# Sixteen more tokens gather their second products, ten pairs of chunks of v go unsplit, and one pool holds the PSUM banks

## The chip, the core and the metric

The kernel runs on one core of a Trainium2 chip. A core has a matrix engine (TensorE, PE in the profile), a vector engine (VectorE, DVE), a scalar engine (ScalarE, ACT), GpSimd (POOL) and a queue engine that only issues DMAs (SyncE, SP). Each engine works through its own list of instructions in order, and semaphores tie the lists together. The metric is the device time of one execution in microseconds, the median of the runs shown.

## What is computed

One layer of a decoder for 256 tokens of width 1024. A mixer (retention and block attention) comes first and isn't touched by the change. Behind it stands a layer of 16384 small experts, 8 heads with 16 experts each for every token:

```python
def peer(h, w_q, sub_keys, u_tab, v_tab):
    ...
    top_s, pos = lax.top_k(cand_s, PEER_TOPK)
    experts = jnp.take_along_axis(cand_i, pos, axis=-1)
    gates = jax.nn.softmax(top_s, axis=-1).astype(h.dtype)
    ...
        u = u_tab[ec]
        a = jax.nn.gelu(jnp.einsum('td,thkd->thk', hc, u), approximate=False)
        return jnp.einsum('thk,thkd->td', gc * a, v_tab[ec])
```

`u_tab` and `v_tab` have 16384 rows of 1024 numbers, in float32. The "first product" of a token and an expert is the dot product with a row of `u_tab`, the "second product" is the weight times a row of `v_tab`, added up over the experts.

## The kernel before

The span has three stages. Up to about 312 us stand the mixer, the projection to the queries and the first scores. Then come two passes over the expert tables in 128 chunks of 128 rows each, first over `u_tab` (312 to 689 us, the loop at L1173), then over `v_tab` (689 to 985 us, the loop at L1224). The order of every engine's instructions is the order in which the program is written, since a manual schedule is set (L76); pieces of side work (a list of generators) are handed out by small budgets per chunk.

**Three kinds of tokens.** The first 64 tokens (NG) gather both products: two partitions stand for a token, and 64 indirect DMAs (NJ) each fetch one row for each of the 128 partitions, 512 KB in all. The next 64 tokens (NX, four groups of 16, eight partitions a token) gather only their first products, with 64 more indirect DMAs; their weights are sent back to the token order through memory (`weights_x`, L965, and `back`, L976). The last 128 tokens gather nothing. So the pass over `u_tab` has NA = 128 columns of tokens, and the pass over `v_tab` has ND = 192.

**The pass over u.** For each chunk TensorE turns the chunk (L681, 8 transposes of 128x128 into PSUM tiles), ScalarE copies it out (L682), and TensorE multiplies it with the tokens (L1188, 8 products of 128 columns, float32). A float32 matmul of the program is two matmul instructions in the trace. `W`, a tile of 128 partitions by 128 chunks by ND tokens, takes the result. Beside this, one-hot factors for four tokens at a time are built on DVE (L1077, L1079) and ACT (L1083), TensorE multiplies them (L1117) into the gates of all experts, and these are multiplied into `W` (L1130, L1132). There are ND/4 = 48 such groups, 8 matmul instructions each. DVE also takes the dot products of the gathered rows (`dot_v`, L962), at `GATHER` or `GATHER_G` steps a chunk.

**The pass over v.** The products are to be exact to about float32, at the faster rate of the type fp32r. So each chunk of v is split in a high part (ACT, L143) and a low part (DVE, L144), and each pair of chunks of `W` in a high and a low part that stand side by side in `cw` (ACT L1161, DVE L1162). For each of eight blocks of 128 output columns, TensorE then does two matmuls: the high part of v with both parts of `W` (L1220, 2 x 192 = 384 columns) and the low part of v with the high part of `W` (L1221, 192 columns). The eight results stay in the eight PSUM banks during the whole pass. The split runs two chunks ahead; its tiles have four buffers. The raw chunks arrive in a ring of six buffers (`RAWS`) by DMAs that SP issues, each as soon as the split has freed its buffer. Beside this, `gather_step` (L1003) fetches rows of v by indirect DMA (L951, issued by POOL) and DVE adds them up with their weights (L1035), `GATHER_V` = 0.56 steps a chunk, with RING = 5 row buffers.

**The end.** The last two chunks are done block by block. Each block is added up (L1257, L1258), turned back (L1263, L1264), added to the residual (L1265, L1266) and written out (L1269, L1270).

**PSUM.** A pool of 4 tiles under each of two names serves up to 312 us (L82). It is closed there (L1062), and three new pools take its banks (L1064 to L1066): `acc` for the products, `gates` and `turn`. They are closed in turn at the end of the pass over u (L1211), and a pool of eight tiles takes over. A tile of a new pool has to wait until every tile that stood in its bank is free.

Of the kernel before, what the change touches and what calls it, by code (L numbers as in the profile page):

```python
# [22 lines left out]
P = 128  # L23
S = 256
# [46 lines left out]
def layer_kernel(ctx, tc, x, mix_norm_g, w_in, ret_w_branch, moba_q_gain, moba_k_gain, moba_w_branch,  # L71
# [10 lines left out]
    psum = {"acc": cps.enter_context(tc.tile_pool(name="ps", bufs=4, space=bass.MemoryType.PSUM))}  # L82
    psum["side"] = psum["acc"]
# [12 lines left out]
    raw_ring = rg.tile([P, RAWS, 1024], F32, name="raw_ring")  # L96
    raw_count = [0]
# [108 lines left out]
    def products(i):  # L206
        u, src, k0, n0 = pieces[i]
        hi, lo = splits.pop(i)
        kc = u["kc"]
        if k0 == 0:  # L210
            if u["before"]:
                u["before"]()
            u["o"] = [acc() for _ in range(2)]
        o = u["o"]
        lh, ll = u["lhs"]
        def parts(j):
            k, n = k0 + j, slice(j * 512, (j + 1) * 512)
            return k, lh[k // 4][:, k % 4, :], ll[k // 4][:, k % 4, :], hi[:, n], lo[:, n]

        if u["mode"] == "nat":  # L220
            for t in range(NT):
                s = slice(t * P, (t + 1) * P)
                for j in range(2):
                    k, xh, xl, wh, wl = parts(j)
                    T.matmul(o[t], xh[:, s], wh, start=(k == 0), stop=False)  # L225
                    T.matmul(o[t], xh[:, s], wl, start=False, stop=False)  # L226
                    T.matmul(o[t], xl[:, s], wh, start=False, stop=(k == kc - 1))  # L227
        else:
            for j in range(2):
                k, xh, xl, wh, wl = parts(j)  # L230
                for b in range(4):
                    s = slice(b * P, (b + 1) * P)
                    d = o[b // 2][:, (b % 2) * S:(b % 2 + 1) * S]
                    T.matmul(d, wh[:, s], xh, start=(k == 0 and b % 2 == 0), stop=False, skip_group_check=True)  # L234
                    T.matmul(d, wh[:, s], xl, start=False, stop=False, skip_group_check=True)  # L235
                    T.matmul(d, wl[:, s], xh, start=False, stop=(k == kc - 1), skip_group_check=True)  # L236
# [434 lines left out]
    def transpose_u(c):  # L671

        if c < NK and c % STEP == STEP - 1 and c // STEP < NPRE:
            u_T[c] = u_raw.pop(c)
        elif c < NK:
            r = u_raw.pop(c)
            u_T[c] = hi_tile(F32)
            for q in range(2):
                p = psum["turn"].tile([P, 512], F32, name="turn") if "turn" in psum else side()
                for k in range(4):  # L680
                    T.transpose(p[:, k * P:(k + 1) * P], r.rearrange("p (i k) -> p k i", k=KC)[:, 4 * q + k], ident)  # L681
                A.activation(u_T[c][:, 512 * q:512 * (q + 1)], p, AF.Copy)  # L682
# [32 lines left out]
    grow1 = [acc() for _ in range(2)]  # L715
# [249 lines left out]
    def weights_x():  # L965
# [37 lines left out]
    def gather_step():  # L1003
# [6 lines left out]
        if gs["dot"] < NU:  # L1010
# [17 lines left out]
        if gs["sum"] < gs["v"] and (gs["v"] - gs["sum"] == RING or gs["v"] == NJ):  # L1028
            j = gs["sum"]
            r = gs["rows"].pop(j)  # L1030
            if j == 0:
                gs["acc"] = cp.tile([P, D], F32, name="vacc", tag="h2")
                A.activation(gs["acc"], r, AF.Copy, scale=av[:, 0:1])
            else:
                V.scalar_tensor_tensor(gs["acc"], r, av[:, j:j + 1], gs["acc"], op0=OP.mult, op1=OP.add)  # L1035
# [57 lines left out]
    def dense_gates():  # L1093

        def columns(t):
            p = psum["turn"].tile([P, 512], F32, name="turn")
# [10 lines left out]
        for n0 in range(0, ND + 4 * LAG_G, 4):  # L1107
# [4 lines left out]
                columns(0)  # L1112
            if len(built) == LAG_G or (n0 >= ND and built):
                n1, oh = built.pop(0)
                p = psum["gates"].tile([P, 512], F32, name="gp")
                for j, (o2, o1) in enumerate(oh[0]):
                    T.matmul(p[:, j * P:(j + 1) * P], o2, o1, start=True, stop=True)  # L1117
# [55 lines left out]
    for c in range(NK):  # L1173
# [34 lines left out]
    product_evac(NK - 2, pa)  # L1208


    cps.close()  # L1211
    psum["acc"] = ctx.enter_context(tc.tile_pool(name="psv", bufs=KC, space=bass.MemoryType.PSUM))

    o = [acc() for _ in range(KC)]
    half = P - NG

    def block(b, c):
        vh, vl, w = cuts[c]
        n = slice(b * P, (b + 1) * P)
        T.matmul(o[b][:, :2 * ND], vh[:, n], w, start=(c == 0), stop=False, skip_group_check=True)  # L1220
        T.matmul(o[b][:, :ND], vl[:, n], w[:, :ND], start=False, stop=(c == NK - 1), skip_group_check=True)  # L1221

    cuts = {}
    for c in range(NK):  # L1224
        load_to(len(pieces) + NK + c + 2)
        cut_v(c + 2)
        if c % 2 == 0:
            cut_w(c + 2)
        cuts[c] = (*v_cut.pop(c), w_cut[c - c % 2][:, c % 2])
        if c < NK - 2:  # L1230
            for b in range(KC):
                block(b, c)
            del cuts[c]
        gather(GATHER_V)
        if c == NK - 8:
            while gs["sum"] < NJ:
                gather_step()

            r0 = tk.tile([P, D], F32, name="rows_")
# [4 lines left out]
            nc.gpsimd.dma_start(r0b[:half], x1d[NG:, 0, :])  # L1244
# [8 lines left out]
    back = {}  # L1253

    def add_up(b):
        lo = back[b] = hp_.tile([P, 2, 2 * P], F32, name="turned", tag="hl", bufs=2)
        A.activation(lo[:, 0, :ND], o[b][:, ND:2 * ND], AF.Copy)  # L1257
        V.tensor_tensor(lo[:, 1, :ND], lo[:, 0, :ND], o[b][:, :ND], op=OP.add)  # L1258

    def turn_back(b):  # L1260
        t = back.pop(b)
        n = slice(b * P, (b + 1) * P)
        T.transpose(o[b][:, :P], t[:, 1, :P], ident)  # L1263
        T.transpose(o[b][:half, P:2 * P], t[:, 1, P:ND], ident)  # L1264
        V.tensor_tensor(r1[:, n], r1[:, n], o[b][:, :P], op=OP.add)  # L1265
        V.tensor_tensor(r0b[:half, n], r0b[:half, n], o[b][:half, P:2 * P], op=OP.add)  # L1266
        if b in (3, 5, 7):
            d = slice({3: 0, 5: 512, 7: 768}[b], P * (b + 1))
            nc.sync.dma_start(out_flat[P:, d], r1[:, d])  # L1269
            (nc.scalar if b == 7 else nc.sync).dma_start(out_flat[NG:P, d], r0b[:half, d])  # L1270
# [62 lines left out]
```

## Time and profile before

| | |
|---|---|
| time, median of 3 runs | 993.85 us (991.02 to 995.42) |
| the profiled execution, its own time | 992.1 us |
| its span, from the first to the last instruction | 990.3 us |
| granted TensorE clock | 1.00 |
| busy: PE, DVE, ACT, POOL | 979.6, 802.9, 551.8, 336.8 us |
| moved by DMA | 309.94 MB, 313 GB/s over the span |

A view of the profile is a list of rows: an engine, a line of the program (L1220), what is written and read, how often, and how long. "Busy" for TensorE has to be read with care, since matmuls are pipelined and overlap: what counts is the distance from one start to the next. The chain of waits is the work that ended last, followed back from the last instruction to what released it. Starts are given in us from the start of the span.

### The profile page before, as it was taken

Reading aid. Unit: us, or ns where it says so; the run is one execution under the profiler, and the core shown is the slowest. Engines: PE = TensorE matmul, PEld = TensorE weight load, DVE = VectorE, ACT = ScalarE, POOL = GpSimd, SP = SyncE. Lnnn points to the kernel's source line nnn. Section 1 sums busy time; section 2 is a strip of 40 time slices with the busy share of each in tenths; the row PEclk is TensorE's granted clock in tenths of the full one; section 3 lists DMA queues with packets and bytes.
Section 4 is the critical chain, followed back from the end, with each engine's and each line's share of the span. In section 5 each row is a group of like instructions: output and inputs, shape, how many; then the busy total and the mean of one; then the engine's idle time right before and its main releaser. Section 6 shows DMA issues by size and latency. Waiting matters only on the chain.

```text
span 990.3 us, 19575 instructions
## 1 busy us (share of the span) xinstructions
PE 979.6 (99%) x7384; PEld 942.9 (95%) x7384; DVE 802.9 (81%) x1509; ACT 551.8 (56%) x992; POOL 336.8 (34%) x287
## 2 busy tenths in 40 slices
PE   9999999999998999999999999999999999999998
PEld 6887998998998999999999999999999999999997
DVE  6567665978679996999688898863999899999976
ACT  5544554535543545444577776986555555555553
POOL 2421000000203455343446565653444344444300
PEclk9999999999999999999999999999999999999999
DMA  8876777996798999999998888999999999999991
GB/s 304 239 198 188 234 226 205 285 305 204 246 375 330 402 352 343 347 363 394 373 342 316 346 333 337 332 390 320 352 360 347 365 363 346 372 351 347 354 284 48
DMA packets 105563, 309.94 MB, mean 313 GB/s; under 512 B 10956, under 2 KB 21093, under 8 KB 105342
## 3 DMA queue, kind: packets, MB, share of 16 engines
q1 hardware_dynamic: 64492, 184.69, 53.1%
q0 software_dynamic: 30240, 107.16, 29.7%
q10 hardware_dynamic: 10738, 16.85, 5.5%
q8 instruction: 58, 0.95, 0.4%
q14 instruction: 35, 0.29, 0.1%
HBM read 298.09 MB, written 12.09 MB: 313 GB/s over the span
## 4 chain that ended last, share of the span: by engine, by line
PE 92%; DVE 3%; DMA 2%; ACT 1%; issue 1%; POOL 0%; ACTq 0%; DVEq 0%; another core or an unknown queue 0%; POOLq 0%
PE acc L1188 21%; PE acc L1220 21%; PE turn L681 9%; PE acc L1221 9%; PE acc L234 4%; PE acc L235 4%; PE acc L236 4%; PE acc L225 4%; PE acc L227 4%; PE acc L226 4%; PE gp L1117 4%; PE side L586 1%; DMA rows<-in_peer_u_dram,eg 1%; DVE rows L962 1%; PE side L356 1%
## 5 line engine op out<-in xcount | busy, mean ns | idle before, releaser
L951 POOL DMA_INDIRECT rows<-in_peer_u_dram,eg x103 | 122.3, 1187 | 93.7 <-DVE rows L962 40.9
L951 POOL DMA_INDIRECT rows<-in_peer_v_dram,eg x51 | 89.3, 1752 | 105.3 <-DVE vacc L1035 100.0
L681 PE MATMUL turn<-ident,raw_ring 128*128 128x128 f32 x816 | 107.1, 274 | 0.0
L681 PEld LDWEIGHTS turn<-ident,raw_ring 128*128 128x128 f32 x816 | 98.7, 190 | 0.0
L962 DVE SCALAR_TENSOR_TENSOR rows<-rows,h 128x1024 f32<-128x1024 f32 x52 | 63.4, 1222 | 21.3 <-DMA rows<-in_peer_u_dram,eg 20.0
L1161 ACT ACTIVATE cw<-W 128x384 fp32r<-128x384 f32 x64 | 33.7, 526 | 81.9 <-PE acc L1221 62.1
L1035 DVE SCALAR_TENSOR_TENSOR vacc<-rows,av,vacc 128x1024 f32<-128x1024 f32 x50 | 64.0, 1280 | 0.0
L1162 DVE TENSOR_TENSOR cw<-W,cw 128x384 fp32r<-128x384 f32 x64 | 36.1, 564 | 20.1 <-ACT cw L1161 18.3
L1132 ACT ACTIVATE W<-gp 128x512 f32<-128x512 f32 (+17 forms) x48 | 33.1, 689 | 32.7 <-DVE W L1130 27.5
L1147 POOL TENSOR_TENSOR W<-W,gl 128x256 f32<-128x256 f32 (+16 forms) x29 | 23.4, 808 | 69.2 <-ACT gl L1146 59.5
L1077 DVE TENSOR_TENSOR oh_buf<-niota,tT 128x512 f32<-128x512 f32 x48 | 34.4, 717 | 7.7 <-ACT tT L1099 7.7
L1130 DVE TENSOR_TENSOR W<-gp,W 128x280 f32<-128x280 f32 (+16 forms) x32 | 29.7, 929 | 4.4 <-PE gp L1117 2.8
L1083 ACT ACTIVATE oh_more<-oh_more,tT 128x128 f32<-128x128 bf16 x96 | 32.1, 428 | 0.0
L1083 ACT ACTIVATE oh_buf<-oh_more,tT 128x128 f32<-128x128 bf16 x96 | 32.1, 428 | 0.0
L541 POOL DMA_DIRECT2D x1d<-xt x1 | 0.7, 657 | 89.3 <-DVE xt L523 89.3
L150 POOL TENSOR_TENSOR gny<-va,minus_half 128x8 f32<-128x8 f32 x2 | 3.3, 1656 | 76.5 <-DVE va L443 76.5
L1188 PE MATMUL acc<-hTf,raw_ring 128*128 128x128 f32 x224 | 27.3, 275 | 0.0
L1117 PE MATMUL gp<-oh_more,oh_buf 128*128 128x128 f32 x192 | 26.0, 278 | 0.3 <-ACT oh_more L1083 0.3
L1188 PEld LDWEIGHTS acc<-hTf,raw_ring 128*128 128x128 f32 x224 | 26.1, 192 | 0.0
L1117 PE MATMUL gp<-oh_buf 128*128 128x128 f32 x192 | 25.5, 276 | 0.0
L1117 PEld LDWEIGHTS gp<-oh_more,oh_buf 128*128 128x128 f32 x192 | 23.9, 192 | 0.5 <-ACT oh_more L1083 0.5
L1117 PEld LDWEIGHTS gp<-oh_buf 128*128 128x128 f32 x192 | 23.5, 192 | 0.0
(2203 smaller groups left out, 3559.4 us busy)
## 6 DMA issues: line engine op xcount, KB each, us to landing
raw_ring<-in_peer_v_dram SPq DMA_DIRECT2D x128, 512.0 KB
raw_ring<-in_peer_u_dram SPq DMA_DIRECT2D x102, 512.0 KB
raw_ring<-in_w_in_dram SPq DMA_DIRECT2D x52, 512.0 KB
raw_ring<-in_peer_w_q_dram SPq DMA_DIRECT2D x16, 512.0 KB
raw_ring<-turned SPq DMA_DIRECT2D x14, 512.0 KB
W<-in_peer_u_dram SPq DMA_DIRECT2D x12, 512.0 KB
raw_ring<-in_ret_w_branch_dram SPq DMA_DIRECT2D x8, 512.0 KB
raw_ring<-in_w_out_dram SPq DMA_DIRECT2D x8, 512.0 KB
```

Of the source, the lines that this page charges most:

```text
L225: T.matmul(o[t], xh[:, s], wh, start=(k == 0), stop=False)
L226: T.matmul(o[t], xh[:, s], wl, start=False, stop=False)
L227: T.matmul(o[t], xl[:, s], wh, start=False, stop=(k == kc - 1))
L681: T.transpose(p[:, k * P:(k + 1) * P], r.rearrange("p (i k) -> p k i", k=KC)[:, 4 * q + k], ident)
L951: G.indirect_dma_start(out=r, out_offset=None, in_=tab, in_offset=bass.IndirectOffsetOnAxis(ap=eg[:, j:j + 1], axis=0))
L962: V.scalar_tensor_tensor(r, r, 1.0, h, op0=OP.mult, op1=OP.mult, accum_out=av[:, j:j + 1])
L1035: V.scalar_tensor_tensor(gs["acc"], r, av[:, j:j + 1], gs["acc"], op0=OP.mult, op1=OP.add)
L1083: A.activation(o1[:, j], o1b[:, :, j], AF.Copy, scale=tT[:, t, 1, k + j:k + j + 1])
L1117: T.matmul(p[:, j * P:(j + 1) * P], o2, o1, start=True, stop=True)
L1188: T.matmul(pa[:, n:n + NA], uT[:, k * P:(k + 1) * P], hTf[:, k], start=(c % 2 == 0 and k == 0), stop=(k == KC - 1), skip_group_check=True)
L1220: T.matmul(o[b][:, :2 * ND], vh[:, n], w, start=(c == 0), stop=False, skip_group_check=True)
L1221: T.matmul(o[b][:, :ND], vl[:, n], w[:, :ND], start=False, stop=(c == NK - 1), skip_group_check=True)
```

## The change

Of the 64 tokens that gather only first products, 16 (NXP x NXV) now gather their second products too. They keep their weights in the layout of the gather, 8 partitions a token; 16 more indirect DMAs fetch their rows of v, ahead of the 64 others (`v_order`), and the weighted rows are added up in a tile of their own, `accx`. Near the end (chunk 123) eight float32 matmuls with a matrix `pick` of 16 columns add up the eight partitions of a token, and put the sums beside the dense results in PSUM. So the dense part of the pass over v has ND = 176 columns, and 44 groups of one-hots.

Ten pairs of chunks of v (`PLAIN`, chunks 8 and 9, 20 and 21, up to 116 and 117) are not split: TensorE multiplies the raw chunk with the raw `W` in float32, one matmul of the program per block (176 columns).

The ring of gathered rows has 6 buffers, and the gather rates per chunk are 0.6, 1.04 and 1.36 in place of 0.56, 1.0 and 1.24. All PSUM tiles come from one pool that is never closed, two buffers each for `acc0` and `acc1` and four for `side`: the turned chunks use `side`, the gates `acc1`, and in the pass over v the eight results take the next buffers of these names. The last write of an output block is two DMAs in place of one.

```diff
-ND = S - NG
+NXV = 1
-NA = ND - NX
-RING = 5
-GATHER_V = 0.56
-GATHER = 1.0
-GATHER_G = 1.24
+NA = S - NG - NX
+NW = NG + NXP * NXV
+ND = S - NW
+RING = 6
+GATHER_V = 0.6
+GATHER = 1.04
+GATHER_G = 1.36
+NV = NJ + NXP * NXV
+PLAIN = [4 + 6 * i for i in range(10)]
...
-    def acc():
-        return psum["acc"].tile([P, 512], F32, name="acc")
+    def acc(i):
+        return psum.tile([P, 512], F32, name="acc", tag=f"acc{i}", bufs=2)
     def side():
-        return psum["side"].tile([P, 512], F32, name="side")
+        return psum.tile([P, 512], F32, name="side", bufs=4)
...
-        if gs["v"] < NJ:
-            fetch(peer_v[0], gs["v"])
+        if gs["v"] < NV:
+            fetch(peer_v[0], v_order[gs["v"]])
...
-    cps.close()
-    cps = ExitStack()
-    psum["acc"] = cps.enter_context(tc.tile_pool(name="psa", bufs=2, space=bass.MemoryType.PSUM))
-    psum["gates"] = cps.enter_context(tc.tile_pool(name="psg", bufs=2, space=bass.MemoryType.PSUM))
-    psum["turn"] = cps.enter_context(tc.tile_pool(name="pst", bufs=4, space=bass.MemoryType.PSUM))
...
-    cps.close()
-    psum["acc"] = ctx.enter_context(tc.tile_pool(name="psv", bufs=KC, space=bass.MemoryType.PSUM))
-    o = [acc() for _ in range(KC)]
+    o = [side() for _ in range(4)] + [acc(i) for i in (1, 1, 0, 0)]
...
         vh, vl, w = cuts[c]
         n = slice(b * P, (b + 1) * P)
+        if vl is None:
+            T.matmul(o[b][:, :ND], vh[:, n], w, start=False, stop=False, skip_group_check=True)
+            return
...
-        cut_v(c + 2)
-        if c % 2 == 0:
-            cut_w(c + 2)
-        cuts[c] = (*v_cut.pop(c), w_cut[c - c % 2][:, c % 2])
+        if (c + 2) // 2 not in PLAIN:
+            cut_v(c + 2)
+            if c % 2 == 0:
+                cut_w(c + 2)
+        if c // 2 in PLAIN:
+            cuts[c] = (v_raw.pop(c), None, W[:, c, :])
+        else:
+            cuts[c] = (*v_cut.pop(c), w_cut[c - c % 2][:, c % 2])
...
+        if c == NK - 5:
+            for b in range(KC):
+                T.matmul(o[b][:, 2 * ND:2 * ND + NXP], accx[:, b * P:(b + 1) * P], pick, start=False, stop=True,
+                         skip_group_check=True)
```

The order shows two places. On TensorE in the pass over v, from chunk 7 on, this stands before (`rhi` and `rlo` are the high and low part of a chunk of v, `cw` the split `W`):

```order
L1220 MATMUL acc<-cw,rhi__7627 128x384
L1221 MATMUL acc<-cw,rlo__7628 128x192
L1220 MATMUL acc<-cw,rhi__7651 128x384
L1221 MATMUL acc<-cw,rlo__7652 128x192
L1220 MATMUL acc<-cw,rhi__7651 128x384
```

And this stands there now; the raw chunks 8 and 9 come between the split chunks 7 and 10:

```order
L1224 MATMUL acc<-cw,rhi__7593 128x352
L1225 MATMUL acc<-cw,rlo__7594 128x176
L1222 MATMUL side<-W,raw_ring 128x176 x4
L1222 MATMUL acc<-W,raw_ring 128x176 x4
L1222 MATMUL side<-W,raw_ring 128x176 x4
L1222 MATMUL acc<-W,raw_ring 128x176 x4
L1224 MATMUL side<-cw,rhi__7651 128x352
L1225 MATMUL side<-cw,rlo__7652 128x176
```

The split pair of matmuls has 352 and 176 columns, and an unsplit chunk is eight matmuls of 176 columns that read `W` and the ring of raw chunks themselves.

On DVE in the pass over v, this stands before (L144 makes the low part of a chunk of v, L1162 that of a pair of chunks of `W`, L1035 adds a gathered row):

```order
L144 TENSOR_TENSOR rlo__7725<-raw_ring,rhi__7724 128x1024
L144 TENSOR_TENSOR rlo__7746<-raw_ring,rhi__7745 128x1024
L1162 TENSOR_TENSOR cw<-W,cw 128x2x192
L1035 SCALAR_TENSOR_TENSOR vacc<-rows__7600,av,vacc 128x1024
L144 TENSOR_TENSOR rlo__7772<-raw_ring,rhi__7771 128x1024
L144 TENSOR_TENSOR rlo__7793<-raw_ring,rhi__7792 128x1024
```

And this stands now around the first unsplit pair, whose work falls between `rlo__7594` and `rlo__7652`:

```order
L147 TENSOR_TENSOR rlo__7568<-raw_ring,rhi__7567 128x1024
L1165 TENSOR_TENSOR cw<-W,cw 128x2x176
L1042 SCALAR_TENSOR_TENSOR accx<-rows,av,accx 128x1024
L147 TENSOR_TENSOR rlo__7594<-raw_ring,rhi__7593 128x1024
L1042 SCALAR_TENSOR_TENSOR accx<-rows,av,accx 128x1024
L147 TENSOR_TENSOR rlo__7652<-raw_ring,rhi__7651 128x1024
```

Two splits of v and one of `W` are gone at each of the ten places, and the sums of gathered rows go on there.

More of the change, by code (lines that the diff above doesn't have):

```diff
@@ L51 @@
 HELD = [0, 1, 2] + list(range(8, 62, 6))
-HELD0 = 20
+HELD0 = 14
 NPRE = 14
@@ L80, in layer_kernel @@
     hp_ = ctx.enter_context(tc.tile_pool(name="hp", bufs=1))
-    cps = ExitStack()
-    psum = {"acc": cps.enter_context(tc.tile_pool(name="ps", bufs=4, space=bass.MemoryType.PSUM))}
-    psum["side"] = psum["acc"]
+    psum = ctx.enter_context(tc.tile_pool(name="ps", bufs=1, space=bass.MemoryType.PSUM))
     dr = ctx.enter_context(tc.tile_pool(name="dr", bufs=1, space=bass.MemoryType.DRAM))
@@ L212, in products @@
                 u["before"]()
-            u["o"] = [acc() for _ in range(2)]
+            u["o"] = [acc(i) for i in range(2)]
         o = u["o"]
@@ L678, in transpose_u @@
             for q in range(2):
-                p = psum["turn"].tile([P, 512], F32, name="turn") if "turn" in psum else side()
+                p = side()
                 for k in range(4):
@@ L714, in layer_kernel @@
         T.transpose(busy[:, i % 4 * P:(i % 4 + 1) * P], ident, ident)
-    grow1 = [acc() for _ in range(2)]
+    grow1 = [acc(i) for i in range(2)]
     for q in range(2):
@@ L834, in layer_kernel @@
     ready = []
+    v_order = [*range(NJ, NV), *range(NJ)]
+    accx = tk.tile([P, D], F32, name="accx")
+    pick = tk.tile([P, NXP], F32, name="pick")
     def x_rows(a, n):
@@ L949, in fetch @@
         gs["n"] += 1
-        r = tk.tile([P, D], F32, name="rows_") if n == 4 else hp_.tile([P, D], F32, name="rows", tag=("hl", "hh")[n % 2], bufs=2)
+        r = tk.tile([P, D], F32, name="rows_", bufs=2) if n >= 4 else hp_.tile([P, D], F32, name="rows", tag=("hl", "hh")[n % 2], bufs=2)
         G.indirect_dma_start(out=r, out_offset=None, in_=tab,
@@ L976, in back @@
         def back():
-            for n in range(NXG):
+            for n in range(NXV, NXG):
                 nc.gpsimd.dma_start(x_rows(gates, n), gx[1][n].rearrange("h i k -> i h k"))
@@ L1024, in gather_step @@
             return
-        if gs["v"] < NJ:
-            fetch(peer_v[0], gs["v"])
+        if gs["v"] < NV:
+            fetch(peer_v[0], v_order[gs["v"]])
             gs["v"] += 1
-        if gs["sum"] < gs["v"] and (gs["v"] - gs["sum"] == RING or gs["v"] == NJ):
-            j = gs["sum"]
+        if gs["sum"] < gs["v"] and (gs["v"] - gs["sum"] == RING or gs["v"] == NV):
+            j = v_order[gs["sum"]]
             r = gs["rows"].pop(j)
-            if j == 0:
-                gs["acc"] = cp.tile([P, D], F32, name="vacc", tag="h2")
-                A.activation(gs["acc"], r, AF.Copy, scale=av[:, 0:1])
-            else:
-                V.scalar_tensor_tensor(gs["acc"], r, av[:, j:j + 1], gs["acc"], op0=OP.mult, op1=OP.add)
+            if j in (0, NJ):
+                gs["acc" if j == 0 else "accx"] = a = cp.tile([P, D], F32, name="vacc", tag="h2") if j == 0 else accx
+                A.activation(a, r, AF.Copy, scale=av[:, j:j + 1])
+            else:
+                a = gs["acc" if j < NJ else "accx"]
+                V.scalar_tensor_tensor(a, r, av[:, j:j + 1], a, op0=OP.mult, op1=OP.add)
             gs["sum"] += 1
     V.tensor_scalar(niota, iota, -1.0, None, op0=OP.mult)
+    V.tensor_reduce(pick, ident.rearrange("p (h i) -> p i h", i=NXP), axis=AX.X, op=OP.add)
     V.tensor_copy(iota4, iota[:, :, None].to_broadcast([P, NK, 4]))
@@ L1095, in columns @@
         def columns(t):
-            p = psum["turn"].tile([P, 512], F32, name="turn")
+            p = side()
             for j, src in enumerate((i12f[:, t, 0], i12f[:, t, 1], gates[:, t])):
@@ L1114, in dense_gates @@
                 n1, oh = built.pop(0)
-                p = psum["gates"].tile([P, 512], F32, name="gp")
+                p = acc(1)
                 for j, (o2, o1) in enumerate(oh[0]):
@@ L1183, in layer_kernel @@
         if c % 2 == 0:
-            pa = acc()
+            pa = acc(0)
         uT = u_T.pop(c)
@@ L1235, in layer_kernel @@
         if c == NK - 8:
-            while gs["sum"] < NJ:
+            while gs["sum"] < NV:
                 gather_step()
-            r0 = tk.tile([P, D], F32, name="rows_")
+            r0 = tk.tile([P, D], F32, name="rows_", bufs=2)
             nc.gpsimd.dma_start(r0[:NG], x1d[:NG, 0, :])
@@ L1255, in add_up @@
     def add_up(b):
-        lo = back[b] = hp_.tile([P, 2, 2 * P], F32, name="turned", tag="hl", bufs=2)
-        A.activation(lo[:, 0, :ND], o[b][:, ND:2 * ND], AF.Copy)
-        V.tensor_tensor(lo[:, 1, :ND], lo[:, 0, :ND], o[b][:, :ND], op=OP.add)
+        t = back[b] = hp_.tile([P, 512], F32, name="turned", tag="hl", bufs=2)
+        A.activation(t[:, :ND + NXP], o[b][:, ND:2 * ND + NXP], AF.Copy)
+        V.tensor_tensor(t[:, :ND], t[:, :ND], o[b][:, :ND], op=OP.add)
     def turn_back(b):
```

14 lines of the change are left out of this document (8 added, 6 removed).

## The prediction

> **What bounds the kernel now.** I read the page's first part, then the stages, then who waits for whom on TensorE. The page's line of busy time, three stages by windows (span, PE, PEld, DVE, ACT, POOL, granted clock, DMA share, GB/s), and the waits of TensorE over the whole span:
>
> ```profile
> PE 979.6 (99%) x7384; PEld 942.9 (95%) x7384; DVE 802.9 (81%) x1509; ACT 551.8 (56%) x992; POOL 336.8 (34%) x287
> ...
> 490.00:575.00 85.00, 85.00 (x763) 85.00 (x763) 75.09 (x128) 61.96 (x177) 43.86 (x39) 1.00 0.91 343
> 575.00:612.00 37.00, 36.68 (x328) 36.49 (x326) 32.85 (x57) 25.82 (x81) 21.41 (x23) 1.00 0.86 325
> ...
> 700.00:929.34 229.34, 229.34 (x1603) 229.34 (x1602) 209.41 (x206) 126.91 (x151) 103.04 (x57) 1.00 0.97 359
> ...
> PE turn L681 <- ACT W L590: 2.6, 1, 2.6
> ...
> PE acc L1220 <- ACT gl L1146: 0.5, 1, 0.5
> ```
>
> TensorE is busy 99% at a granted clock of 1.00. A busy TensorE need not be at its pace, so I looked at starts in the pass over v. The first matmul of chunk 1 and the first of chunk 125, in the timeline:
>
> ```profile
> 691.66 0.36 PE L1220 MATMUL acc<-cw,rhi__7489 128*128 128x384 f32 x1
> ...
> 976.03 0.36 PE L1220 MATMUL acc<-cw,rhi__10404 128*128 128x384 f32 x1
> ```
>
> 124 chunks in 284.37 us are 2.293 us a chunk, or 286.7 ns for each of its eight pairs of matmuls. The waits name none for TensorE in between. The kernel is bound by what TensorE issues, and the change is worth what it takes from that list, as long as DVE (209.41 of 229.34 us) and the DMAs (share 0.97) keep up.
>
> **The change, part by part.** Each sum goes against the profiled execution, 992.1 us with a span of 990.3; the median is 1.75 us above it.
>
> *Split chunks, 108 of them.* A pair goes from 384 + 192 to 352 + 176 columns. What is a column worth? Steps of plain streams: the chain of waits for 512 columns (start, us until the next; 13 steps lie between these rows), the timeline for 256 (18 steps):
>
> ```profile
> 59.98 0.23 PE acc L227
> ...
> 62.92 0.23 PE acc L225
> ...
> 257.78 0.28 PE L236 MATMUL acc<-hh,rlo__2388 128*128 128x256 f32 x1
> ...
> 259.94 0.28 PE L236 MATMUL acc<-hh,rlo__2405 128*128 128x256 f32 x1
> ```
>
> That is 226.2 and 120.0 ns, so 0.415 ns a column and 13.8 ns a matmul. By this the old pair would take 173 + 93.5 = 266.6 ns; it takes 286.7. Something adds 20 ns. The timeline of one pair with its weight loads:
>
> ```profile
> 700.18 0.25 PE L1221 MATMUL acc<-cw,rlo__7558 128*128 128x192 f32 x1
> 700.18 0.19 PEld L1220 LDWEIGHTS acc<-cw,rhi__7557 128*128 128x128 f32 x1
> ...
> 700.26 0.36 PE L1220 MATMUL acc<-cw,rhi__7557 128*128 128x384 f32 x1
> 700.29 0.19 PEld L1221 LDWEIGHTS acc<-cw,rlo__7558 128*128 128x128 f32 x1
> ```
>
> The load for the 384-column matmul starts together with the 192-column matmul, and the next load 0.11 us later. And streams of float32 matmuls of 64 (L381) and of 128 columns (L1188), in the chain of waits:
>
> ```profile
> 67.22 1.73 PE side L381 x16
> ...
> 683.39 5.37 PE acc L1188 x48
> ```
>
> 108 and 112 ns a matmul: half the columns, nearly the same step. So I read a floor of about 110 ns, the time of a weight load, under every matmul. The 192-column matmul lies on it (93.5 by its columns), 173 + 113 = 286. Shrinking it further gives nothing; only the 384-column one gains, 32 x 0.415 = 13.3 ns. The new pair takes 273.4 ns, a chunk 2.187 us: 108 x 8 x 13.3 ns = **-11.5 us**. Ends: without a floor 48 x 0.415 = 19.9 ns, -17.2 us; and nothing below -11.5 on the other side, unless the floor rises.
>
> The Trainium skill, "TensorE: Matmul & The Clock Gate", section "Back-to-back issue gap", has the isolated spacing go by columns alone, 2.4 to the ns and 2.5 ns a matmul; by it the pair loses 20 ns, -17.3 us. Its section "LDWEIGHTS (loading the stationary operand)" puts 128 columns of weights at 107 ns, and with that the second matmul has a floor. This trace, with 286.7 ns for a pair, speaks for the second.
>
> *Unsplit chunks, 20 of them.* One float32 matmul of 176 columns is two instructions. The step at 256 columns, in the timeline:
>
> ```profile
> 113.57 0.38 PE L407 MATMUL side<-rv,kdec 128*128 128x256 f32 x1
> ...
> 113.79 0.38 PE L407 MATMUL side<-rv,kdec 128*128 128x256 f32 x1
> ```
>
> 215 ns for 256 columns and 112 for 128 give 151 for 176 by a straight line; 16 instructions are 2.41 us a chunk against 2.293: 20 x 0.117 = **+2.3 us**. Ends: by proportion to 256 columns (148 ns) +1.5; the other way, if switching types costs a load each time, +4. This part is a loss on TensorE; what it frees is DVE (below).
>
> *The sums of the gather.* Eight float32 matmuls of 16 columns lie on the floor: 16 x 112 ns = **+1.8 us** (ends 0.9 to 2.5). Their operand is finished long before chunk 123.
>
> *One-hot groups.* Four of 48 go; the chain of waits has for each:
>
> ```profile
> 670.92 0.89 PE gp L1117 x8
> ```
>
> 4 x 0.89 = **-3.6 us**; the DVE and ACT work of these groups goes with them.
>
> *One PSUM pool.* At 312.8 us TensorE waits 2.6 us (the wait above), because the first turned chunk takes a bank of a new pool, and that waits for the score tiles. The timeline of this place:
>
> ```profile
> 311.04 2.05 PE L586 MATMUL side<-skT,W 128*128 128x128 f32 x16
> ...
> 311.93 1.32 ACT L682 ACTIVATE rhi__3129<-side 128x512 f32<-128x512 f32 x2 [0.16 <-PE side L681]
> ...
> 314.15 1.49 ACT L590 ACTIVATE W<-side,r 128x512 f32<-128x512 f32 x2 [0.90 <-PE side L586]
> ...
> 315.69 1.16 PE L681 MATMUL turn<-ident,W 128*128 128x128 f32 x8 [2.60 <-ACT W L590]
> ```
>
> In the ring of four `side` tiles the two score tiles are the youngest, and the next turned chunk takes the two before, which ACT empties at 313.25. So TensorE goes on at about 313: **-2.4 us**, ends 0 and -2.6. Next late is chunk 3, whose tiles are the score tiles, free at 315.64, just when it comes. At 689 us the 0.5 us goes as well, since the first blocks take turned tiles that have long been emptied: **-0.5**.
>
> *Gather pace in the pass over u.* 1.36 steps in place of 1.24, add 0.12 dot products a chunk. A chunk there is 8 turned blocks, 16 instructions of products and 8 of one-hots at 0.112 us, 3.57 us; from 490 to 612 us these are 34 chunks. A dot product and the other DVE work of the pass over v, rows by line (mean ns, then idle before):
>
> ```profile
> 700.25 1.23 DVE L144 TENSOR_TENSOR rlo__7628<-raw_ring,rhi__7627 128x1024 fp32r<-128x1024 f32 x1 [0.39 <-ACT rhi__7627 L143]
> ...
> L962 DVE SCALAR_TENSOR_TENSOR rows<-rows,h 128x1024 f32<-128x1024 f32 x52 | 63.4, 1222 | 21.3 <-DMA rows<-in_peer_u_dram,eg 20.0
> L1035 DVE SCALAR_TENSOR_TENSOR vacc<-rows,av,vacc 128x1024 f32<-128x1024 f32 x50 | 64.0, 1280 | 0.0
> L1162 DVE TENSOR_TENSOR cw<-W,cw 128x384 fp32r<-128x384 f32 x64 | 36.1, 564 | 20.1 <-ACT cw L1161 18.3
> ```
>
> 34 x 0.12 x 1.22 = 5 us, and DVE is idle 85 - 75.1 + 37 - 32.9 = 14 us there: it fits, but TensorE already loses 0.3 us in 575 to 612. I take **+0.8**, ends 0 and 4. The sixth buffer of the ring helps against late rows.
>
> *The last write.* One more DMA is issued behind the last one on ACT's queue:
>
> ```profile
> 987.04 0.54 ACTq L1270 DMA_DIRECT2D out_dram<-oh_more  x1
> ```
>
> **+0.5 us** (0 to 0.6).
>
> *Does DVE keep up in the pass over v?* Twelve chunks need now 12 x 1.23 + 6 x 0.56 + 12 x 0.56 x 1.28 = 26.7 us of DVE in 27.5 of TensorE. After: ten splits, five of `W` (0.52 each, by its columns), 7.2 sums: 24.1 us, against 10 x 2.187 + 2 x 2.41 = 26.7 of TensorE, 90%. In a run of ten split chunks DVE needs 2.26 us a chunk against 2.187, and falls back 0.7 us. Its lead covers that. Low part 8 starts at 702.59 on DVE, and TensorE first uses it at 707.9:
>
> ```profile
> 702.59 1.22 DVE L144 TENSOR_TENSOR rlo__7652<-raw_ring,rhi__7651 128x1024 fp32r<-128x1024 f32 x1
> ...
> L1221 PE MATMUL acc<-cw,rlo__7652 x8: 250/250/250, 707.9 to 709.9; 128*128 128x192 f32 x8
> ```
>
> That is a lead of almost 4 us. I count nothing. Without that cover, ten runs of 0.7 would cost 7 us. Without the unsplit pairs DVE would need these 2.26 us for every chunk of 2.187 and set the pace, so they pay for the rest.
>
> *Do the DMAs keep up?* A chunk of 0.524 MB and 0.56 gathers of the same size in 2.293 us are 357 GB/s (the window says 359). After, 1.6 x 0.524 MB in 2.225 us are 377. In the pass over u a stretch had more:
>
> ```profile
> 320.00:350.00 30.00, 30.00 (x271) 30.00 (x271) 29.73 (x119) 14.00 (x28) 12.29 (x12) 1.00 1.02 401
> ```
>
> 401 GB/s for 30 us, with TensorE never idle. I count nothing.
>
> Sum: -11.5 + 2.3 + 1.8 - 3.6 - 2.4 - 0.5 + 0.8 + 0.5 = -12.6 us. 992.1 - 12.6 = 979.5; from the median it is 981.2. I forecast 980.
>
> **The rivals.**
>
> *No floor* (17%). If the 20 ns come from something else, the pair loses 19.9 ns and the split chunks give -17.2: 974. For it: the matmul of 384 columns starts 0.08 us after the one of 192, less than a load. Against it: 64 columns cost as much as 128.
>
> *Given back in the pass over u* (12%). If the opening waits as before (the pool then does not do what it is there for) and the faster dots cost TensorE 4 us in the one-hots, then -12.6 + 2.4 + 3.2 = -7: 985. For it: DVE at 88% and TensorE's first losses there.
>
> *DMA at its ceiling* (7%). If the pass over v gets no more than the 359 GB/s it had, a chunk takes 0.839 MB / 359 = 2.337 us, 0.112 more, for the 118 chunks with gathers 13 us: 992.6, no change. The Trainium skill, "DMA: Bandwidth & Descriptors", section "Where 436 GB/s comes from", sets about 358 GB/s for reads from HBM, which speaks against this change; the 401 GB/s above go against it as a limit for one core alone.
>
> *Slower: DMA below its old rate* (6%). More of the traffic are gathers, 0.6 of 1.6 in place of 0.56 of 1.56, and an unsplit chunk frees its raw buffer only when TensorE is done. If the mix is delivered at 345, the chunk takes 2.43 us: +24 us, 1004. It decides from about 359 GB/s down; the row of 401 speaks against.
>
> **How the numbers follow.** A change under 0.5%, 5 us, can hardly be told from none. The forecast (977 to 984) has 58%, no floor 17%, given back 12%: these are faster, together 0.87. DMA at its ceiling is the same, 0.07; slower 0.06. The range leaves out the two DMA cases, 13%, and a little at each end: 972 (no floor with the other gains at their best ends) to 988 (given back, with the unsplit chunks at +4).
>
> **What would show it right or wrong.** A split chunk takes 2.19 us between the first matmuls (2.13 without a floor), an unsplit one 2.41; the pass over v lasts about 8 us less; no wait at 313 and at 689 us; 44 one-hot groups; no waits of TensorE for low parts or raw chunks. Waits on a DMA in the pass over v, at 345 to 359 GB/s, would make the prediction wrong, as would more than 4 us of waits for one-hots between 490 and 640 us.

## The result, and the profile after

The changed kernel takes 977.87 us (median of 6 runs, 975.41 to 981.07), the kernel before, run beside it, 994.3 us (6 runs, 991.02 to 995.42). The ratio is 0.984 [0.982, 0.986], so 1.6% less time, clear of the noise; 980 was forecast. The profiled execution took 978.6 us with a span of 976.8, so 13.5 us less than the one of before, where the sum said 12.6. The medians differ by 16.4 us; for the 3 us between, no profile shows a place.

The page's line of busy time, and three stages by windows (columns as in the prediction):

```profile
PE 968.4 (99%) x7368; PEld 931.0 (95%) x7368; DVE 782.1 (80%) x1487; ACT 516.5 (53%) x943; POOL 364.0 (37%) x303
```

```profile
490.00:575.00 85.00, 84.58 (x759) 84.42 (x758) 77.31 (x139) 62.98 (x185) 50.63 (x44) 1.00 0.97 370
575.00:612.00 37.00, 36.81 (x324) 36.42 (x323) 32.08 (x54) 22.61 (x70) 23.61 (x22) 1.00 0.88 329
697.00:941.20 244.20, 243.68 (x1760) 243.35 (x1759) 203.57 (x201) 114.57 (x136) 107.60 (x67) 1.00 0.98 375
```

TensorE is still busy 99% of the span. In the pass over v DVE fell to 83% (203.57 of 244.20 us), and the DMAs deliver 375 GB/s where 377 were counted. The largest waits of TensorE over the whole span:

```profile
PE side L717 <- DVE ident L707: 1.5, 1, 1.5
PE side L1224 <- DVE cw L1165: 0.5, 1, 0.5
PE side L733 <- DVE hn L730: 0.5, 2, 0.3
PE side L684 <- DMA raw_ring<-in_peer_u_dram: 0.4, 1, 0.4
```

The 2.6 us at 313 and the 0.5 us at 689 are gone. A wait for `cw` in the pass over v is new. Where each part of the time went is read from the timeline of TensorE, from the opening of the pass over u on:

```profile
309.13 1.97 PE L684 MATMUL side<-ident,W 128*128 128x128 f32 x16
310.94 2.25 PE L589 MATMUL side<-skT,W 128*128 128x128 f32 x16
313.03 1.05 PE L684 MATMUL side<-ident,W 128*128 128x128 f32 x8
313.91 0.83 PE L1191 MATMUL acc<-hTf,rhi__3119 128*128 128x128 f32 x6
...
685.82 0.36 PE L1224 MATMUL side<-cw,rhi__7458 128*128 128x352 f32 x1
...
701.08 1.39 PE L1222 MATMUL side<-W,raw_ring 128*128 128x176 f32 x8
...
703.50 1.36 PE L1222 MATMUL side<-W,raw_ring 128*128 128x176 f32 x8
...
714.58 0.35 PE L1224 MATMUL side<-cw,rhi__7732 128*128 128x352 f32 x1
...
714.77 0.24 PE L1225 MATMUL side<-cw,rlo__7733 128*128 128x176 f32 x1
...
714.85 0.36 PE L1224 MATMUL side<-cw,rhi__7732 128*128 128x352 f32 x1
...
959.07 0.99 PE L1259 MATMUL side<-pick,accx 128*128 128x16 f32 x8
959.91 1.04 PE L1259 MATMUL acc<-pick,accx 128*128 128x16 f32 x8
...
963.03 0.36 PE L1224 MATMUL side<-cw,rhi__10131 128*128 128x352 f32 x1
```

Four readings. The third turned chunk starts at 313.03, right behind the score tiles, and the first products at 313.91 in place of 316.69. The first matmul of chunk 1 of the pass over v stands at 685.82, that of chunk 125 at 963.03: 277.21 us, 7.2 less than before. A split pair steps by 0.27 us (714.58 to 714.85), and the median of all split chunks is 2.181 us. An unsplit chunk takes 2.42 us (701.08 to 703.50), and the second of a pair 2.27; the split chunk behind it loses another 0.10. The eight sums of the gather, 16 instructions of only 16 columns, step by 0.84 / 8 = 105 ns; chunk 123, in which they stand, takes 3.92 us, 1.74 more than the others, 109 ns for each of the 16.

One chunk, number 75, takes 3.00 us. ACT's timeline just ahead of it:

```profile
847.52 1.06 ACT L146 ACTIVATE rhi__9054<-raw_ring 128x1024 fp32r<-128x1024 f32 x1 [3.70 <-DMA raw_ring<-in_peer_v_dram]
```

ACT waited 3.7 us for a raw chunk, the low parts behind it came late, and TensorE lost 0.8 us. SP's own waits say what had held the raw chunks back:

```profile
SPq L637 <- PE acc L1222: 84.9, 20, 7.7
```

SP issues the raw chunks in order, each when its buffer is free, and an unsplit chunk frees its buffer only when TensorE has multiplied it. So no raw chunk is issued between 829.34 and 836.59 us, where the first chunk of the unsplit pair 68 and 69 ends, and then six follow within 5.8 us.

The difference of the two spans then goes in three pieces. Up to the first product of the pass over v the changed kernel is 5.7 us ahead (683.59 against 689.29; the prediction's terms for this stretch make -3.6 - 2.4 - 0.5 + 0.8 = -5.7): 2.8 at the opening, 2.1 in the pass over u, 0.8 at the change to v. From there to chunk 125 it wins 7.3 us, and in the tail 0.5.

### The profile page after: what moved, and what is told of

The parts are those of the page before. It is cut to its first block, busy times and chain, and to the rows that moved or that the text cites. A ratio compares the mean times of both kernels' runs of the same rounds, so it can differ in the third digit from the quotient of the medians.

```text
span 976.8 us, 19439 instructions
## 1 busy us (share of the span) xinstructions
PE 968.4 (99%) x7368; PEld 931.0 (95%) x7368; DVE 782.1 (80%) x1487; ACT 516.5 (53%) x943; POOL 364.0 (37%) x303
## 4 chain that ended last, share of the span: by engine, by line
PE 93%; DMA 2%; DVE 2%; ACT 1%; issue 1%; POOL 0%; ACTq 0%; SPq 0%; DVEq 0%; POOLq 0%
PE acc L1191 22%; PE side L684 10%; PE acc L1224 8%; PE side L1224 8%; PE acc L237 4%; PE acc L238 4%; PE acc L239 4%; PE acc L228 4%; PE acc L1120 4%; PE acc L230 4%; PE acc L229 4%; PE acc L1225 4%; PE side L1225 4%; PE side L1222 2%; PE acc L1222 2%; DMA raw_ring<-in_peer_u_dram 2%
## 5 line engine op out<-in xcount | busy, mean ns | idle before, releaser
L957 POOL DMA_INDIRECT rows<-in_peer_u_dram,eg x86 | 107.9, 1254 | 76.3 <-DVE rows L968 34.9
L684 PE MATMUL side<-ident,raw_ring 128*128 128x128 f32 x816 | 107.2, 274 | 0.5 <-DMA raw_ring<-in_peer_u_dram 0.4
L684 PEld LDWEIGHTS side<-ident,raw_ring 128*128 128x128 f32 x816 | 98.7, 191 | 0.9 <-issue 0.9
L1135 ACT ACTIVATE W<-acc 128x512 f32<-128x512 f32 (+17 forms) x44 | 28.1, 639 | 35.7 <-DVE W L1133 31.7
L1164 ACT ACTIVATE cw<-W 128x352 fp32r<-128x352 f32 x54 | 26.6, 492 | 25.4 <-PE acc L1225 21.6
L1165 DVE TENSOR_TENSOR cw<-W,cw 128x352 fp32r<-128x352 f32 x54 | 28.1, 520 | 6.3 <-ACT cw L1164 6.3
L1133 DVE TENSOR_TENSOR W<-acc,W 128x280 f32<-128x280 f32 (+16 forms) x32 | 24.6, 768 | 4.8 <-PE acc L1120 3.7
L1222 PE MATMUL side<-W,raw_ring 128*128 128x176 f32 x160 | 27.4, 314 | 0.0
L1222 PE MATMUL acc<-W,raw_ring 128*128 128x176 f32 x160 | 27.1, 313 | 0.0
L1042 DVE SCALAR_TENSOR_TENSOR accx<-rows,av,accx 128x1024 f32<-128x1024 f32 x9 | 11.9, 1324 | 17.6 <-ACT accx L1039 11.2
L1222 PEld LDWEIGHTS acc<-W,raw_ring 128*128 128x128 f32 x160 | 24.7, 190 | 0.0
```

Of the source, the lines that this page charges most:

```text
L957: G.indirect_dma_start(out=r, out_offset=None, in_=tab, in_offset=bass.IndirectOffsetOnAxis(ap=eg[:, j:j + 1], axis=0))
L1042: V.scalar_tensor_tensor(a, r, av[:, j:j + 1], a, op0=OP.mult, op1=OP.add)
L1222: T.matmul(o[b][:, :ND], vh[:, n], w, start=False, stop=False, skip_group_check=True)
```

## The experiments

Four questions: whether every matmul really has a floor, whether the unsplit pairs pay, what the pool and the gather rates are worth, and how much room DVE and the DMAs have. Ratios are to the kernel before, run on the same chip.

**The floor under the second matmul.** Two kernels change its columns and nothing else; here is the one with 240, the other has 64 in its place.

```diff
-        T.matmul(o[b][:, :ND], vl[:, n], w[:, :ND], start=False, ...)
+        T.matmul(o[b][:, :240], vl[:, n], w[:, :240], start=False, ...)
```

> The changed kernel with the second matmul of a split pair (low part of v) over 240 columns in place of 176; the 64 more columns add terms to the result that do not belong there. My theory, a floor of a weight load under each matmul: 240 columns are 13.8 + 240 x 0.415 = 113 ns, just the floor, so the pair stays at 273 ns, the chunk at 2.18 us and the time at 978. Rival, no floor: 64 x 0.415 = 27 ns more a pair, 108 x 8 x 27 ns = +23 us, 1001.

> The changed kernel with the second matmul of a split pair over 64 columns in place of 176; the other 112 columns are left out of the result. My theory, the floor: the pair stays at 273 ns within a chunk, and the time at 978. Rival, no floor: 112 x 0.415 = 46 ns less, pairs of 227 ns within a chunk, and the time falls until DVE sets the pace, to about 965 to 970.

Measured: with 240 columns 978.5 us (975.84 to 979.41), ratio 0.986 [0.985, 0.988], and a split chunk of 2.20 us. With 64 columns 976.29 us in its only run, and a chunk of 2.19. The timeline of pairs, first of 64 columns, then of 240:

```profile
714.43 0.40 PE L1224 MATMUL acc<-cw,rhi__7732 128*128 128x352 f32 x1
714.67 0.20 PE L1225 MATMUL acc<-cw,rlo__7733 128*128 128x64 f32 x1
714.70 0.40 PE L1224 MATMUL acc<-cw,rhi__7732 128*128 128x352 f32 x1
```

```profile
714.51 0.32 PE L1224 MATMUL side<-cw,rhi__7755 128*128 128x352 f32 x1
714.67 0.27 PE L1225 MATMUL side<-cw,rlo__7756 128*128 128x240 f32 x1
714.78 0.32 PE L1224 MATMUL side<-cw,rhi__7755 128*128 128x352 f32 x1
```

From one 352-column start to the next it is 0.27 us both times, as with 176 columns. Nearly four times the columns cost 0.01 us a chunk, so the rival without a floor is out. The two starts inside a pair shift (0.24 and 0.03 us, against 0.16 and 0.11): only the step of the whole pair says what it costs. The Trainium skill, "TensorE: Matmul & The Clock Gate", section "LDWEIGHTS (loading the stationary operand)", gives 107 ns for 128 columns of weights; the 105 to 109 ns a matmul of 16 columns takes in the change agree with it. That the load is what makes the floor stays an argument from this size: no run changes the load.

**The unsplit pairs.** One kernel splits all pairs, one leaves five unsplit, one puts ten unsplit pairs into the kernel before.

```diff
-PLAIN = [4 + 6 * i for i in range(10)]
+PLAIN = []
```

> The changed kernel with no unsplit pair (all 128 chunks split, PLAIN empty). My theory: TensorE alone would gain 20 x (2.39 - 2.18) = 4 us, but DVE needs 1.23 + 0.26 + 0.77 = 2.26 us a chunk against 2.18 of TensorE and sets the pace for the 118 chunks with gathers: +9 - 4 = +5 us, 983, with waits of TensorE for low parts and a chunk of about 2.26 us. Rival: DVE overlaps its instructions enough to keep up, the unsplit pairs are a plain loss, and the time is 974 with chunks of 2.18 us.

Measured: 972.41 us, ratio 0.979 [0.978, 0.981]. Every split chunk takes 2.18 us, and none but chunk 123 is longer. The theory was wrong, and the rival held. The window of the pass over v, and a stretch of DVE in its timeline:

```profile
697.00:941.20 244.20, 244.20 (x1794) 244.20 (x1793) 234.36 (x236) 141.70 (x169) 129.17 (x67) 1.00 1.00 385
```

```profile
719.93 0.53 DVE L1165 TENSOR_TENSOR cw<-W,cw 128x352 fp32r<-128x352 f32 x1 [0.36 <-ACT cw L1164]
720.37 1.28 DVE L1042 SCALAR_TENSOR_TENSOR vacc<-rows,av,vacc 128x1024 f32<-128x1024 f32 x1
721.57 1.22 DVE L147 TENSOR_TENSOR rlo__7880<-raw_ring,rhi__7879 128x1024 fp32r<-128x1024 f32 x1
722.70 1.21 DVE L147 TENSOR_TENSOR rlo__7901<-raw_ring,rhi__7900 128x1024 fp32r<-128x1024 f32 x1
724.29 0.52 DVE L1165 TENSOR_TENSOR cw<-W,cw 128x352 fp32r<-128x352 f32 x1 [0.37 <-ACT cw L1164]
```

The rows overlap: the split at 721.57 lasts 1.22 us, and the next starts at 722.70, 1.13 later. By starts a split costs 1.136 us, a half pair of `W` 0.436 and a term of the sum 1.196, so a chunk needs 1.136 + 0.218 + 0.6 x 1.196 = 2.07 us of DVE, less than the 2.18 of TensorE, and DVE even waits for ACT in between.

```diff
-PLAIN = [4 + 6 * i for i in range(10)]
+PLAIN = [6 + 12 * i for i in range(5)]
```

> The changed kernel with five unsplit pairs in place of ten (every twelfth pair from the sixth). My theory: 24 chunks need 22 x 1.23 + 11 x 0.52 + 14.4 x 1.28 = 51 us of DVE in 22 x 2.18 + 2 x 2.39 = 52.7 us of TensorE, so TensorE still sets the pace and ten chunks get 0.21 us shorter: -2 us, 976. Rival: ten pairs are needed, runs of 22 split chunks use up the lead of DVE of 4 us, and the time is 979 to 982.

Measured: 975.41 us, ratio 0.983 [0.981, 0.984], 3.0 us above the kernel with all pairs split on the same chip; from the change, 0.984 [0.982, 0.986], it can't be told. Its profile has one late chunk as well, number 115, which takes 3.89 us:

```profile
PE side L1224 <- DVE cw L1165: 3.9, 2, 2.6
```

The kernel with ten unsplit pairs beside the old sizes (`PLAIN` and its three uses in the diff of the change, nothing else):

> The kernel before with the ten unsplit pairs alone (192 columns, 64 first-product tokens as before). My theory: an unsplit chunk is 16 instructions of 0.112 + 64 x 0.00078 = 0.162 us, 2.59 us against 2.293: 20 x 0.30 = +6 us, 1000. Rival: the relief of DVE is worth something by itself, and the time is 994 or less.

Measured: 996.51 us, ratio 1.0064 [1.0049, 1.0079], 6.3 us more. The timeline of TensorE at a pair:

```profile
706.00 5.39 PE L1222 MATMUL acc<-W,raw_ring 128*128 128x192 f32 x32
711.09 0.47 PE L1224 MATMUL acc<-cw,rhi__7688 128*128 128x384 f32 x1
```

Two unsplit chunks take 5.09 us (706.00 to 711.09) where two split ones take 4.59, and the next chunk loses 0.1. So the float32 chunks are a loss in both kernels, and nothing pays for them.

The change and the kernel with all pairs split, side by side on one chip:

> The changed kernel with all pairs of W split, this time beside the changed kernel on one chip. Theory: a split chunk takes 2.18 us of TensorE and an unsplit one 2.39 (2.34 and what the next chunk loses), so twenty chunks give back 20 x 0.21 = 4.2 us, and with the hitch of 0.8 us that the unsplit pairs had about 5: a ratio of 0.979 against the kernel before, 0.005 below the changed kernel. Rival: the difference seen so far (972.4 and 977.9, on two chips) is the chip's or the run's; then both stand within 1.5 us.

> The changed kernel itself. Theory: 0.984 of the kernel before, as in its first runs, and 4 to 5 us above the kernel with all pairs split. Rival: within 1.5 us of it.

Measured: 973.08 us (972.38 to 973.92), ratio 0.979 [0.978, 0.980], and 977.16 us (975.88 to 978.68), ratio 0.983 [0.982, 0.984]. The runs do not overlap; the unsplit pairs cost 4.1 us. With all pairs split, the kernel is the fastest of all that were run.

**How much room DVE has.** All pairs split, and one more small addition for DVE in each chunk, whose output nobody reads.

```diff
-PLAIN = [4 + 6 * i for i in range(10)]
+PLAIN = []
...
+        if c < NK - 8:
+            V.tensor_tensor(oh_more[:, 0, c % 4], tT[:, 0, 0], tT[:, 0, 1], op=OP.add)
```

> All pairs split, and one more DVE addition of 128 columns in each of the first 120 chunks of the pass over v. Theory: DVE's need goes by the steps from start to start, 1.136 us for a split of a raw chunk, 0.436 for half of a pair of W split, 1.196 for a term of the gather's sum: 1.136 + 0.218 + 0.6 x 1.196 = 2.07 us a chunk. The steps of 1024 and of 352 columns give 1.04 ns a column and 0.07 us fixed, so 0.20 us for 128: 2.27 us a chunk against 2.18 of TensorE. DVE then sets the pace, less the lead of some 4 us that it starts with: 120 x 0.09 - 4 to 120 x 0.09, so 7 to 11 us more than with all pairs split, 979 to 983, with waits of TensorE for low parts. Rival: DVE has more room than the steps say (the added one slips into its gaps); then TensorE still sets the pace, a chunk stays at 2.18 and the time within 2 us of all pairs split.

Measured: 981.1 us (979.73 to 982.18), ratio 0.987 [0.986, 0.989]: 8.0 us more than with all pairs split. The window of the pass over v, and the waits of TensorE there:

```profile
697.00:941.20 244.20, 238.96 (x1735) 236.60 (x1734) 244.20 (x335) 137.17 (x164) 219.30 (x64) 1.00 0.99 369
```

```profile
PE side L1224 <- DVE cw L1165: 5.2, 9, 0.6
```

DVE is busy all 244.20 us, and TensorE waits. The first chunks still take 2.18 us; from chunk 31 on, when the lead is used up, one chunk in ten takes 2.95, and ten chunks together lose 0.92. Ten chunks of 0.09 us too much DVE work make 0.9. So the sum by starts is right to a few hundredths of a us, and with all pairs split DVE has 0.1 us a chunk to spare, not more.

**The pool alone.** The kernel before, with the one pool and the banks of the change.

```diff
-    psum["turn"] = cps.enter_context(tc.tile_pool(name="pst", bufs=4, ...))
...
-                p = psum["turn"].tile([P, 512], F32, name="turn") if "turn" in psum else side()
+                p = side()
...
-    o = [acc() for _ in range(KC)]
+    o = [side() for _ in range(4)] + [acc(i) for i in (1, 1, 0, 0)]
```

> The kernel before with one PSUM pool that is never closed (tiles acc0, acc1, side as in the change) and nothing else. My theory: the wait of 2.6 us at 313 us and the one of 0.5 us at 689 us go: -2.9 us, 991.4 against 994.3. Rival: the wait comes back elsewhere (chunk 3 takes the score tiles, or one-hots wait for DVE), and the time stays within 0.5 us.

Measured: 988.87 us (11 runs), ratio 0.9984 [0.9975, 0.9993]: 1.6 us less, 0.7 to 2.5. Its timeline at the opening:

```profile
311.03 1.95 PE L584 MATMUL side<-skT,W 128*128 128x128 f32 x16
312.82 1.05 PE L679 MATMUL side<-ident,W 128*128 128x128 f32 x8
313.70 1.95 PE L1181 MATMUL acc<-hTf,rhi__3116 128*128 128x128 f32 x16
```

The wait at 313 is gone as in the change, and the products start 3.0 us earlier than in the profile of before. But the wait is not 2.6 us in every execution of the old pools. The kernel before with the ten unsplit pairs has the same program up to the pass over v, and ran on the same chip as this one. Its timeline at the opening:

```profile
313.81 1.16 PE L682 MATMUL turn<-ident,W 128*128 128x128 f32 x8 [0.78 <-ACT W L591]
314.81 1.95 PE L1189 MATMUL acc<-hTf,rhi__3116 128*128 128x128 f32 x16
```

It waits 0.8 us there. Against this profile the one pool is 1.1 us ahead at the first products of the pass over u and 1.7 at the first product of the pass over v (685.85 for 687.57), just what the timed runs show. From the first to the last product of the pass over u the three profiles with the old rates take 371.8, 372.0 and 372.1 us, so nothing is given back there. Why the wait differs from one execution to another is open.

**The gather rates.** The change with the old rates in the passes over u.

```diff
-GATHER = 1.04
-GATHER_G = 1.36
+GATHER = 1.0
+GATHER_G = 1.24
```

> The changed kernel with the gather rates of the pass over u set back to 1.0 and 1.24 steps a chunk (the rate of the pass over v stays at 0.6). My theory: the dot products end about 8 sums later, these are left over at chunk 120 and are done there in one go, 8 x 1.28 = 10 us of DVE against a lead of 4: +6 us, 984, with a wait of TensorE behind chunk 120. Rival: the faster rates cost TensorE about 1 us between 490 and 620 us and buy nothing: 977.

Measured: 992.9 us (987.75 to 993.91), ratio 1.0022 [1.0010, 1.0033]. All that the change wins is lost, three times what was expected. The longest wait of TensorE, its granted clock around it (the column before the last two), and DVE's timeline near the end:

```profile
PE side L1225 <- DVE rlo__10089 L147: 10.6, 1, 10.6
...
940.00:968.00 28.00, 17.44 (x114) 17.19 (x112) 24.40 (x23) 7.74 (x10) 11.64 (x11) 0.83 0.87 281
```

```profile
947.91 3.93 DVE L1042 SCALAR_TENSOR_TENSOR vacc<-rows,av,vacc 128x1024 f32<-128x1024 f32 x3
951.87 1.28 DVE L1042 SCALAR_TENSOR_TENSOR vacc<-rows__10012,av,vacc 128x1024 f32<-128x1024 f32 x1
953.42 1.28 DVE L1042 SCALAR_TENSOR_TENSOR vacc<-rows__10036,av,vacc 128x1024 f32<-128x1024 f32 x1 [0.26 <-DMA rows__10036<-in_peer_v_dram,eg]
955.84 3.92 DVE L1042 SCALAR_TENSOR_TENSOR vacc<-rows,av,vacc 128x1024 f32<-128x1024 f32 x3 [1.14 <-DMA rows<-in_peer_v_dram,eg]
961.63 1.28 DVE L1042 SCALAR_TENSOR_TENSOR vacc<-rows,av,vacc 128x1024 f32<-128x1024 f32 x1 [1.86 <-DMA rows<-in_peer_v_dram,eg]
962.83 1.22 DVE L147 TENSOR_TENSOR rlo__10089<-raw_ring,rhi__10088 128x1024 fp32r<-128x1024 f32 x1
```

At chunk 120 the program runs the gather to its end (a loop behind the rates), and nine sums are left over. They stand ahead of the next split in DVE's list, wait for their own rows, and take 15 us; TensorE waits 10.6 of them. Behind the wait TensorE runs at a granted clock of 0.50 until 968 us, and a pair takes 0.51 us (964.42 to 964.93) in place of 0.27. The profiled execution, 987.75 us, is the shortest of the nine and has the highest mean clock, 0.995; the other eight have 0.988 to 0.993 and take 989.16 to 993.91. So about two thirds of the loss stand in this profile, and the rest goes with a lower clock, as far as the runs show. In the change the same place has one sum, because the first of the second products come before the pass over v begins. Its timeline there on DVE, the first and the last of eight:

```profile
662.46 1.28 DVE L1042 SCALAR_TENSOR_TENSOR accx<-rows,av,accx 128x1024 f32<-128x1024 f32 x1 [11.18 <-ACT accx L1039]
...
680.01 1.28 DVE L1042 SCALAR_TENSOR_TENSOR accx<-rows__7314,av,accx 128x1024 f32<-128x1024 f32 x1 [1.16 <-DMA rows__7314<-in_peer_v_dram,eg]
```

120 chunks at 0.6 are 72 of the 80 steps; the faster dot products make room for the other eight. With the old rates none of these sums lies ahead of the pass over v.

**How much room the DMAs have.** The change, and in each of the first 120 chunks 128 KB more, read from the table and written over a tile that nobody reads any more.

```diff
+        if c < NK - 8:
+            extra = oh_more.rearrange("p a b i -> p (a b i)")[:, 256 * (c % 4):256 * (c % 4 + 1)]
+            nc.scalar.dma_start(extra, peer_u[0, c * P:(c + 1) * P, :256])
```

> The changed kernel with one more DMA of 128 KB for each of the first 120 chunks of the pass over v, from ACT's queue into a tile that nobody reads. This measures how far the DMAs are from their ceiling. The need goes from 377 to 436 GB/s. My theory: the ceiling is near 405 GB/s, so a chunk takes 0.970 MB / 405 = 2.40 us: +0.175 x 120 = +21 us, 999, with TensorE waiting for raw chunks. Rival, a ceiling well above: 978. Rival, a ceiling of 359 as the pass before had: 0.970 / 359 = 2.70 us, 1035.

Measured: 1004.62 us (1001.32 to 1005.81), ratio 1.0133 [1.0114, 1.0152]. The window of the pass over v, and the first waits of TensorE:

```profile
697.00:941.20 244.20, 231.40 (x1606) 226.19 (x1605) 187.61 (x184) 105.94 (x127) 90.25 (x61) 0.99 1.03 397
```

```profile
PE side L1224 <- DVE cw L1165: 5.8, 12, 1.0
PE side L1224 <- ACT rhi__10040 L146: 2.3, 1, 2.3
```

1.6 x 0.524 + 0.131 = 0.97 MB a chunk would be 436 GB/s at 2.225 us. The window gave 397, and 0.97 MB / 397 is 2.44 us: the pass took 2.47 a chunk. So the DMAs set the pace there, at 397 GB/s, and TensorE's waits show it only at second hand, as late `cw` and late high parts. The change at 375 and the kernel with all pairs split at 385 are 6% and 3% below that.

## Why the prediction was right, and which of its steps weren't

**The split chunks** carried it. The floor was read rightly: 2.187 us was forecast for a chunk, 2.181 measured, -11.8 for -11.2 us over the 105 split chunks up to chunk 125. The two kernels with other widths show the floor itself.

**The unsplit chunks** cost 2.34 us each and 0.1 in the chunk behind, together 2.39 on the mean for the 2.41 forecast. To that comes the one late chunk, 0.8 us. The prediction had named the unsplit chunk's raw buffer, freed only when TensorE is done, and SP's waits show that it holds the next raw chunks back, 20 times. It makes TensorE late only now and then: leaving out the run with more DMA, three of the seven profiles with unsplit pairs have one late chunk each and four have none, as have the two with all pairs split.

**The sums of the gather** took 1.74 us for 1.8, the **opening** gave 2.8 us for 2.4 against this profile of before, and the **tail** won 0.5 where about 0.2 was to be lost; the second DMA of the last write shows no cost there. That the sum comes within 1 us of the profile is in part luck, since the opening and the pass over u differ by 2 to 3 us from one execution to another.

**Failed: "Without the unsplit pairs DVE would need these 2.26 us for every chunk of 2.187 and set the pace, so they pay for the rest."** The step added up durations (1.23, 0.52, 1.28). Instructions that follow one another on DVE overlap by 0.08 us, and by starts the need is 2.07. The kernel with all pairs split is 4.1 us faster than the change, and the added small instruction shows the limit where the sum by starts puts it. The number of the forecast did not hang on this step, since it counted nothing for DVE either way; its verdict on what is useful in the change did.

**Mis-sized: the one pool.** -2.9 us was counted; alone it is worth 1.6 (0.7 to 2.5). The stall at 313 does go, but the term took its 2.6 us from one execution, and another, of a kernel with the same program up to there, has 0.8.

**Incomplete: the gather pace.** +0.8 us was counted for what the faster dots cost TensorE. From the first product of the pass over u to the last, the changed kernel takes 369.65 us for 371.79, so -2.1 with the groups' -3.6, which leaves +1.4 for all else, inside the 0 to 4. But this one profile can't size the term: nine profiles with the change's pass over u take 366.9 to 369.8 us, and the one with the old rates 366.9. What the prediction missed is what the faster rates carry: eight sums that would stand in one go on DVE before the end, 18 us by the ratios, the lower clock behind them included. No rival had it, because the change as made avoids it.

**The DMAs.** "I count nothing" held: 375 GB/s were delivered. The Trainium skill, "DMA: Bandwidth & Descriptors", section "Where 436 GB/s comes from", would have set about 358, as the share of one of two cores; the window of 697 to 941 us has 375, and the measurement decides. But the row of 401 on which the step rested was taken in another mix, and the room was small: with 0.131 / 0.839 = 16% more bytes a chunk the time is 29 us longer by the ratios.

## What to carry to other kernels

Price an engine's work by the distance between starts, not by the durations in the profile, wherever it is close to the pace of another; 0.08 us an instruction decided here whether a part of the change helped or hurt. Where a matmul has its own weights, look for the floor under it before counting on fewer columns. Where side work is handed out at a rate, count steps times rate to the end of the loop: what is left over runs in one go, ahead of work that others wait for.

## What the runs showed of the hardware

- A float32 or fp32r matmul with a 128-column weight load of its own has a floor of some 110 ns: 64, 176 and 240 columns cost the same within 0.02 us a chunk beside a 352-column one, and 16 columns alone take 105 to 109. By the prediction's line through 256 and 512 columns, 240 x 0.415 + 13.8 = 113 ns, the columns should take over at about 240; that is an estimate.
- On DVE, 1024 columns of float32 last 1.22 us in the records and step by 1.136; 352 columns last 0.52 and step by 0.436.
- With 128 KB more a chunk in the pass over v, one core's DMAs gave 397 GB/s over 244 us, at a share of 1.03.
- Behind a wait of 10.6 us, TensorE's granted clock was 0.50 until 968 us, and a pair took 0.51 us in place of 0.27.
